# Two-layer short-conv and retention trunk: the engines' order taken from a timeline simulation, and the first head's norm spread eight steps behind its sums

## The chip, the cores and the metric

One core of a Trainium2 chip. The metric is device microseconds (us) of one execution of the whole program. TensorE is called PE here (PEld: its weight loads), VectorE DVE, ScalarE ACT, GpSimd POOL and SyncE SP. The kernel before takes 1546.74 us, the median of 3 runs (1546.3 to 1547.41).

## The reference

x is (1, 512, 1024) in float32; 16 learned rows are put in front of it, which makes T = 528 rows, and taken away at the end. Each of two layers computes:

```python
def layer(h, p):
    u = rmsnorm(h, pre_norm_g) @ w_in + b_in          # 1024 -> 10240 columns
    # a gated short convolution (3 taps) on 4 x 1024 of the columns
    a = (gb * conv(gc * hh) * silu(z)) @ w_conv_out
    # retention: 4 heads, q and k of 256, v and gate of 512 columns each
    out = decayed_scores(rope(q), rope(k)) @ v
    out = group_norm(out) * silu(z_r)                 # per head and row, over 512
    b = out @ w_ret_out
    y = (sigmoid(g_a) * a + sigmoid(g_b) * b) @ w_o
    return h + rmsnorm(y, post_norm_g)
```

The group norm of a head is the step that the change moves: it needs a sum over the head's 512 values for every row, the power -1/2 of it, and that number at every partition before the head's output can be scaled.

## The kernel before, in words

Everything is held transposed: 1024 features lie on partitions as 8 blocks of 128, and the 528 rows are the free dimension, mostly cut in two halves of 264 (HALF). Every product of float32 matrices is made of three matmuls of a high and a low part: a CAST on ACT makes the high part (L140, `whi`, `Xh`, `r`), a subtraction on DVE the low part (L141, `wlo`, `Xl`, `r`), PE multiplies high by high, high by low and low by high. Weights are loaded as `raw` (SP's queue) and split by those same two lines.

Most of w_in's columns go through `Group` (L283 is its matmul): a Strassen-like scheme with 7 products of 12 matmuls, into the PSUM banks `pa`, `pb`, `pc`; DVE adds weight blocks for it (L311, L318, L319), and ACT evicts the banks (L329, L339). The first columns of layer 0 and some of layer 1 go through `Std` (L672): 8 feature blocks times 3 matmuls for each half, 48 matmuls for 128 columns, into a pair of banks that is copied out by L1023 in layer 0. `pp` is a pool of two PSUM pairs that the scores (L425), the transposes of v (L454), the norms (L374, L388) and other products share in turn: a third user waits until the first one's contents have been read.

A head of retention is k and q, rotated by DVE (rope, L407 to L409: two products and an add or a subtraction, `f<-f,f`), split for PE; scores (L425 on PE, times the decay by L436 on DVE, split by L444 and L445); v transposed (L454) and split by L461, L462 and L467; then `attend` (L486), and the norm in three steps: the sums over partitions by matmuls with a column of ones (L374), scaled by DVE (`nv`, L378), raised to -1/2 by POOL (`ny`, L379); the spread over the partitions by a matmul with `ident` (L388), copied out by ACT (L391); and the scaling of the head's output (L520). The first head of each layer starts it with `z_done(...)` at L1071 and L1090, the others inside `Group`'s callbacks.

What sets the order: the program is written as a list of jobs for PE; `later(d, f)` puts a piece of other work d ticks ahead, and every 12 or so matmuls of PE are one tick (`tick()`), at which what is due is issued. For a norm, `d` is the tick of the sums, and the spread was due at `d + 3`, the scaling at `d + 3 + v`. On top of that the framework (`tile.TileContext`, L1298) puts each engine's instructions in its own order when the program is built, by a simulation that starts with the order of the code and lets pieces marked `tc.high_priority()` (evictions mostly) go first. Every engine then runs its list in order, and waits where an input isn't there or a buffer isn't free.

At the layer change, `wo_half` multiplies by w_o (L672, `wos` and `r` as weights), ACT evicts each product as `YB` (L763) and squares it (L663), DVE adds the squares into `ysum` (L665); `norms` takes the sums (L374), spreads them (L388), scales `YB` (L776), adds the residual (L781), squares and sums again into `hsum` (L663, L665), spreads, scales (L785) and splits `YB` into `Xh`, `Xl` or `r`. All that is done for each half of the rows, and `opening` (L672, `pp_10129` and others) begins layer 1 with the result.

Of the kernel before, what the change touches and what calls it, by code (L numbers as in the profile page):

```python
# [56 lines left out]
def trunk(ctx: ExitStack, tc: tile.TileContext, xT, w_in, binT, w_co, w_ro, w_o, gpre, gpost,  # L57
          gpost_row, convw, convb, gng, cosT, sinT, decay, out):
    nc = tc.nc
# [65 lines left out]
    def later(delay, fn):  # L125
        now[1] += 1
        heappush(queue, (now[0] + delay, now[1], fn))
# [690 lines left out]
    jobs, shut = [], [[False], [False]]  # L818
    entry = [[{}, {}], [{}, {}]]
    for l in range(DEPTH):  # L820
# [7 lines left out]
        hd = heads(0)  # L828
# [56 lines left out]
                for j in range(len(JT)):  # L885
                    later(d + 2 * j, lambda j=j: vtrans(vt, hd["v8"], V, (j,)))

        def z_done(ts, hd, h, l, yr, silu=(1,), d=11):
            cs = slice(QCOLS[l].t0, T)
            for n in silu:  # L890
                later(1, lambda n=n: nc.scalar.activation(ts[n][:, cs], ts[n][:, cs], AF.Silu))
            hd["zt"] = hd.get("zt", []) + list(ts)
            if len(hd["zt"]) < 4:
                return

            def start():
                hd["sums"] = fslot()
                hd["n"] = normed(l, hd["zt"], hd["sums"], yr)
            later(0, start)
            for v in range(4):  # L900
                later(1 + 2 * v, lambda v=v: attend(l, h, *hd["S"], hd["V"], v, hd["zt"][v], hd["sums"]))
            later(d, lambda: hd["n"][0]())
            later(d + 3, lambda: hd["n"][1]())
            for v in range(4):
                later(d + 3 + v, lambda v=v: hd["n"][2](v))

        hd["done"] = (k_done, q_done, v_done, z_done)
        yrs = jb["yrs"] = [[] for _ in range(H)]
# [7 lines left out]
        for h in range(1, H):  # L916
            d = {}
# [150 lines left out]
    for b, half, j in ((A11, 0, 0), (A12, 0, 4), (A22, 1, 4)):  # L1068
        for kk in range(0, 4, 2):
            split(Xh[:, b, kk:kk + 2], Xl[:, b, kk:kk + 2], YH[:, j + kk:j + kk + 2, half, :])  # L1070
    later(14, lambda: z_done(zt, jobs[0][0]["hd"], 0, 0, jobs[0]["yrs"][0], (), 16))  # L1071

    for l in range(DEPTH):
        last = l == DEPTH - 1
# [3 lines left out]
        if l:  # L1078
            hd = jb[0]
            k_done(opened[0:2], hd["hd"])  # L1080
            hd["z"][0].run(0, biased_silu)
            block_sums(0)
            hd["z"][0].run(1, biased_silu)
            block_sums(1)
            q_done(opened[6:8], hd["hd"], 0, 1, 12)
            hd["z"][1].run(0, biased_silu)
            v_done(opened[2:6], hd["hd"], 9)
            hd["z"][1].run(1, biased_silu)
            zt = hd["z"][0].ts + hd["z"][1].ts
            later(14, lambda zt=zt: z_done(zt, jobs[1][0]["hd"], 0, 1, jobs[1]["yrs"][0], (), 16))  # L1090
        wo = jb["wo"].wo
        co = 0

# [208 lines left out]
```

## Time and profile before

| | |
|---|---|
| median of 3 runs | 1546.74 us (1546.3 to 1547.41) |
| the profiled execution | 1547.21 us |
| its span, first to last instruction | 1545.1 us |
| mean granted TensorE clock | 0.997 |
| PE busy | 1527.5 us, 99% |
| PEld busy | 1484.1 us, 96% |
| DVE busy | 1164.2 us, 75% |
| ACT busy | 910.5 us, 59% |
| POOL busy | 30.6 us, 2% |

The profile is of one execution. Its own time lies 0.5 us above the median, and its span 2.1 us below its own time. A row of the timeline gives the start, the duration, the engine, the line, the operation, what it writes and reads, how many alike stand in it, and in brackets the idle time before it with what ended that. Instructions of one engine overlap a little, so the step from one row's start to the next is shorter than the duration.

### The profile page before, as it was taken

How to read it: one execution, taken by the hardware profiler on the slowest of the kernel's cores; microseconds unless marked ns; L12 is line 12 of the kernel's file. 1: busy time of each engine (PE TensorE's matmuls, PEld its weight loads, DVE VectorE, ACT ScalarE, POOL GpSimd, SP SyncE). 2: the span in 40 equal slices, each digit the busy share in tenths (PEclk: the TensorE clock that was granted, in tenths of full speed). 3: DMA queues.
4: the chain of work that ended last, by engine and by line, in shares of the span. 5: the costliest groups of instructions: out<-in, count | busy, mean ns of one | idle time of the engine just before them, and what ended most of it. 6: DMA issues, size and time to landing. Idle time of an engine off the chain costs nothing.

```text
span 1545.1 us, 29345 instructions
## 1 busy us (share of the span) xinstructions
PE 1527.5 (99%) x11762; PEld 1484.1 (96%) x11762; DVE 1164.2 (75%) x1702; ACT 910.5 (59%) x1764; POOL 30.6 (2%) x31
## 2 busy tenths in 40 slices
PE   9998999999999999999999999999999999999998
PEld 9998999999999999999999999999999999999986
DVE  6997776886978788856376988769779777997642
ACT  7684666565465466755345766665755655776531
POOL 0001000000000000000000000000000000000000
PEclk9999999999999999999999999999999999999999
DMA  8132223323232334335331233332322223333431
GB/s 273 55 131 89 96 95 105 113 101 103 89 117 89 104 123 137 130 130 181 122 105 55 98 109 110 117 103 96 123 96 100 100 96 123 132 135 138 139 102 55
DMA packets 86041, 174.38 MB, mean 113 GB/s; under 512 B 11281, under 2 KB 15889, under 8 KB 85905
## 3 DMA queue, kind: packets, MB, share of 16 engines
q1 hardware_dynamic: 85760, 172.50, 32.9%
q8 instruction: 92, 1.51, 0.4%
q14 instruction: 45, 0.36, 0.1%
q10 hardware_dynamic: 144, 0.01, 0.0%
HBM read 168.21 MB, written 4.26 MB: 112 GB/s over the span
## 4 chain that ended last, share of the span: by engine, by line
PE 93%; DVE 3%; ACT 1%; DMA 1%; issue 1%; POOL 0%; SPq 0%; DVEq 0%; POOLq 0%; ACTq 0%
PE pb L283 30%; PE pp L248 18%; PE pc L283 15%; PE pp L672 7%; PE pa L283 7%; PE pp L486 4%; PE pb L672 3%; PE pp L425 2%; PE pp L1164 2%; PE pp L454 1%; PE pp L388 1%; DVE wlo L141 1%; DMA raw<-in_w_in 1%; PE pp L374 1%; POOL ny L379 0%
## 5 line engine op out<-in xcount | busy, mean ns | idle before, releaser
L140 ACT CAST whi<-raw 128x1024 fp32r<-128x1024 f32 (+2 forms) x358 | 339.8, 958 | 234.8 <-PE pp L248 62.9
L141 DVE TENSOR_TENSOR wlo<-raw,whi 128x1024 fp32r<-128x1024 f32 (+2 forms) x358 | 393.6, 1107 | 111.8 <-ACT whi L140 110.1
L283 PE MATMUL pb<-Xh,whi 128*128 128x264 f32 (+2 forms) x1008 | 290.7, 288 | 3.1 <-ACT pa L339 1.6
L283 PE MATMUL pb<-Xl,whi 128*128 128x264 f32 (+2 forms) x1008 | 285.7, 283 | 0.0
L283 PE MATMUL pb<-Xh,wlo 128*128 128x264 f32 (+2 forms) x1008 | 285.7, 283 | 0.0
L248 PE MATMUL pp<-r,whi 128*128 128x264 f32 (+1 forms) x1152 | 244.4, 321 | 0.0
L283 PEld LDWEIGHTS pb<-Xh,whi 128*128 128x128 f32 x1008 | 190.4, 189 | 4.8 <-ACT pa L339 2.2
L283 PE MATMUL pc<-Xh,whi 128*128 128x264 f32 (+2 forms) x672 | 192.2, 286 | 0.9 <-ACT f L329 0.9
L248 PEld LDWEIGHTS pp<-r,whi 128*128 128x128 f32 x1152 | 176.8, 188 | 15.4 <-ACT whi L140 0.3
L283 PEld LDWEIGHTS pb<-Xl,whi 128*128 128x128 f32 x1008 | 190.4, 189 | 0.7
L283 PE MATMUL pc<-Xl,whi 128*128 128x264 f32 (+2 forms) x672 | 190.4, 283 | 0.0
L283 PEld LDWEIGHTS pb<-Xh,wlo 128*128 128x128 f32 x1008 | 190.2, 189 | 0.0
L283 PE MATMUL pc<-Xh,wlo 128*128 128x264 f32 (+2 forms) x672 | 190.1, 283 | 0.0
L248 PE MATMUL pp<-r,wlo 128*128 128x264 f32 (+1 forms) x576 | 153.3, 321 | 0.0
L311 DVE TENSOR_TENSOR raw<-raw 128x512 f32<-128x512 f32 x168 | 114.9, 687 | 37.6 <-DMA raw<-in_w_in 35.2
L283 PEld LDWEIGHTS pc<-Xh,whi 128*128 128x128 f32 x672 | 126.5, 188 | 1.5 <-ACT f L329 1.4
L283 PEld LDWEIGHTS pc<-Xl,whi 128*128 128x128 f32 x672 | 126.5, 188 | 0.1
L283 PEld LDWEIGHTS pc<-Xh,wlo 128*128 128x128 f32 x672 | 126.3, 188 | 0.0
L248 PEld LDWEIGHTS pp<-r,wlo 128*128 128x128 f32 x576 | 95.5, 188 | 8.4
L283 PE MATMUL pa<-Xh,whi 128*128 128x264 f32 (+2 forms) x336 | 96.3, 287 | 0.0
L283 PE MATMUL pb<-Xh,whd 128*128 128x264 f32 (+2 forms) x336 | 95.3, 284 | 1.0 <-ACT f L329 1.0
L318 DVE TENSOR_TENSOR raw<-raw,raw 128x512 f32<-128x512 f32 x84 | 57.9, 689 | 50.6 <-DMA raw<-in_w_in 50.2
(257 smaller groups left out, 3335.5 us busy)
## 6 DMA issues: line engine op xcount, KB each, us to landing
raw<-in_w_in SPq DMA_DIRECT2D x426, 256.0 KB, 2.9
raw<-in_w_ro SPq DMA_DIRECT2D x32, 512.0 KB, 3.3
raw<-in_w_in SPq DMA_DIRECT2D x20, 512.0 KB, 5.2
raw<-in_w_co SPq DMA_DIRECT2D x16, 512.0 KB, 3.3
raw<-in_w_o SPq DMA_DIRECT2D x16, 512.0 KB, 4.0
Dsb<-in_decay SPq DMA_DIRECT2D x8, 520.0 KB, 4.6
h1d<-f SPq DMA_DIRECT2D x8, 264.0 KB, 5.6
f<-h1d SPq DMA_DIRECT2D x8, 264.0 KB, 4.3
```

The costliest lines, as they stand in the source:

```text
L140: nc.scalar.copy(dst_hi, src)
L141: nc.vector.tensor_tensor(dst_lo, src, dst_hi.bitcast(F32), op=ALU.subtract)
L248: nc.tensor.matmul(banks[i][:, 0:cols.n], wt(k)[:, msl], xs(k)[:, sl], start=(k == 0 and a == 0), stop=(k == nk - 1 and a == 2),)
L283: nc.tensor.matmul(o[:, 0:n], wt[:, k, :], xs[:, blk, k, HALF - n:], start=(first and k == 0 and a == 0), stop=(k == 3 and a == 2), skip_g ...
L311: nc.vector.tensor_tensor(r[:, 512:], r[:, 512:], r[:, 0:512], op=ALU.add)
L318: nc.vector.tensor_tensor(b[:, 0:512], a[:, 512:], c[:, 0:512], op=ALU.add)
L374: nc.tensor.matmul(pp[0:sc, 0, c:c + 1], sums[:, t0 + c * sc:t0 + (c + 1) * sc], ones_d[:, 0:1], start=True, stop=True)
L388: nc.tensor.matmul(pp[:, c // per, (c % per) * sc:(c % per + 1) * sc], y[:, c:c + 1].to_broadcast([sc, P]), ident[0:sc, 0:sc], start=True, ...
L425: nc.tensor.matmul(pp[0:kn, n + i, 0:cols.n], k[dt][x][:, k0:k0 + kn] if j < 4 else k8[:, dt * 2 + x, :], q[dt][y][:, sl], start=(dt == 0 ...
L486: nc.tensor.matmul(pp[:, b, lo_ - banks[b][0]:hi_ - banks[b][0]], V[j][x][0:kn, v * P:(v + 1) * P], S[0:kn, SOFF[j] + lo_ - q0:SOFF[j] + h ...
L672: nc.tensor.matmul(o, wt(k), xs[:, i0:], start=(k == 0 and a == 0), stop=(k == KD - 1 and a == 2))
L1164: nc.tensor.matmul(o, x[:, xs], wo[k][half][w], start=(k == 0 and a == 0), stop=(k == KD - 1 and a == 2))
```

## The change

`z_done` gets one more argument, `e`, the ticks between a norm's sums and its spread (3 as before if it isn't given). The first heads of both layers are called with sums 13 ticks ahead instead of 16, and the spread 8 ticks behind them instead of 3, so it is due at 21 instead of 19. And `TileContext` is called with `schedule_with_timeline_sim=True`: the framework makes each engine's order by its timeline simulation instead of its default one. This last line moves instructions in the whole program.

```diff
--- before.py
+++ after.py
@@ -885,7 +885,7 @@
                 for j in range(len(JT)):
                     later(d + 2 * j, lambda j=j: vtrans(vt, hd["v8"], V, (j,)))
 
-        def z_done(ts, hd, h, l, yr, silu=(1,), d=11):
+        def z_done(ts, hd, h, l, yr, silu=(1,), d=11, e=3):
             cs = slice(QCOLS[l].t0, T)
             for n in silu:
                 later(1, lambda n=n: nc.scalar.activation(ts[n][:, cs], ts[n][:, cs], AF.Silu))
@@ -900,9 +900,9 @@
             for v in range(4):
                 later(1 + 2 * v, lambda v=v: attend(l, h, *hd["S"], hd["V"], v, hd["zt"][v], hd["sums"]))
             later(d, lambda: hd["n"][0]())
-            later(d + 3, lambda: hd["n"][1]())
+            later(d + e, lambda: hd["n"][1]())
             for v in range(4):
-                later(d + 3 + v, lambda v=v: hd["n"][2](v))
+                later(d + e + v, lambda v=v: hd["n"][2](v))
 
         hd["done"] = (k_done, q_done, v_done, z_done)
         yrs = jb["yrs"] = [[] for _ in range(H)]
@@ -1068,7 +1068,7 @@
     for b, half, j in ((A11, 0, 0), (A12, 0, 4), (A22, 1, 4)):
         for kk in range(0, 4, 2):
             split(Xh[:, b, kk:kk + 2], Xl[:, b, kk:kk + 2], YH[:, j + kk:j + kk + 2, half, :])
-    later(14, lambda: z_done(zt, jobs[0][0]["hd"], 0, 0, jobs[0]["yrs"][0], (), 16))
+    later(14, lambda: z_done(zt, jobs[0][0]["hd"], 0, 0, jobs[0]["yrs"][0], (), 13, 8))
 
     for l in range(DEPTH):
         last = l == DEPTH - 1
@@ -1087,7 +1087,7 @@
             v_done(opened[2:6], hd["hd"], 9)
             hd["z"][1].run(1, biased_silu)
             zt = hd["z"][0].ts + hd["z"][1].ts
-            later(14, lambda zt=zt: z_done(zt, jobs[1][0]["hd"], 0, 1, jobs[1]["yrs"][0], (), 16))
+            later(14, lambda zt=zt: z_done(zt, jobs[1][0]["hd"], 0, 1, jobs[1]["yrs"][0], (), 13, 8))
         wo = jb["wo"].wo
         co = 0
 
@@ -1295,7 +1295,7 @@
     args = [nc.dram_tensor(f"in_{n}", a.shape, mybir.dt.from_np(a.dtype), kind="ExternalInput").ap()
             for n, a in arrays.items()]
     args.append(nc.dram_tensor("out_y", (SEQ, D), F32, kind="ExternalOutput").ap())
-    with tile.TileContext(nc) as tc:
+    with tile.TileContext(nc, schedule_with_timeline_sim=True) as tc:
         trunk(tc, *args)
     r = run_bass_kernel_spmd(nc, [{f"in_{n}": a for n, a in arrays.items()}], core_ids=[0])
     return r.results[0]["out_y"].reshape(1, SEQ, D)
```

**The first head's norm, on PE.** `ones_d` against `f` are the sums, `ny` is the spread, the L283 rows are products of `Group`. Before:

```order
L374 MATMUL pp_1936<-ones_d,f_1525 88x1 x6
L283 MATMUL pb_1885<-Xh,whi_1787 128x264
...
L283 MATMUL pa_104<-Xh,whi_1787 128x264
...
L283 MATMUL pc_1886<-Xh,whi_1839 128x264
...
L283 MATMUL pc_1886<-Xh,wlo_1840 128x264
L388 MATMUL pp_2009<-ident,ny_1944 128x88 x6
L283 MATMUL pb_1885<-Xh,whi_1839 128x264
```

and now:

```order
L374 MATMUL pp_1875<-ones_d,f_1525 88x1 x6
L283 MATMUL pb_1896<-Xh,whi_1721 128x264
...
L283 MATMUL pc_1897<-Xh,whi_1721 128x264
...
L283 MATMUL pb_1729<-Xh,whd_1661 128x264
...
L283 MATMUL pb_1729<-Xh,wld_1662 128x264
L388 MATMUL pp_2046<-ident,ny_1883 128x88
L283 MATMUL pb_1896<-Xh,whi_1787 128x264
...
L283 MATMUL pb_2031<-Xh,wlo_1889 128x264
L388 MATMUL pp_2046<-ident,ny_1883 128x88 x5
L283 MATMUL pc_2032<-Xh,whi_1888 128x264
```

Before and now, 36 matmuls of L283 stand between the sums and the first matmul of the spread; now the other five of the spread stand 60 matmuls further down. (A line of "..." leaves out rows of the same product.)

**The first head's rope, on ACT and DVE.** `f_778` and `f_795` are the two rotated halves of k, `pp_765` the PSUM pair with the second half of the columns of q. ACT before:

```order
L1027 ACTIVATE f_408<-f_408,bin_92 128x528
L1027 ACTIVATE f_411<-f_411,bin_92 128x528
L140 CAST whi_928<-raw_513 128x1024
L140 CAST r_812<-f_778 128x528
L140 CAST r_828<-f_795 128x528
L1023 COPY f_843<-pp_765 128x264 x2
L1027 ACTIVATE f_414<-f_414,bin_92 128x528
L1027 ACTIVATE f_518<-f_518,bin_92 128x528
```

ACT now:

```order
L140 CAST Xh<-f_690 128x528
L140 CAST whi_995<-raw_516 128x1024
L1027 ACTIVATE f_758<-f_758,bin_92 128x528
L140 CAST r_812<-f_778 128x528
L140 CAST r_828<-f_795 128x528
L140 CAST whd_1286<-t_1214 128x512
L1023 COPY f_843<-pp_765 128x264 x2
L396 CAST r_869<-r_812 128x128
```

DVE before, up to the second rotated half:

```order
L407 TENSOR_TENSOR f_795<-f_408,sin_sb 128x528
L409 TENSOR_TENSOR f_778<-f_778,f_779 128x528
L408 TENSOR_TENSOR f_796<-f_411,cos_sb 128x528
L141 TENSOR_TENSOR wlo_833<-raw_449,whi_832 128x512
L409 TENSOR_TENSOR f_795<-f_795,f_796 128x528
L141 TENSOR_TENSOR r_813<-f_778,r_812 128x528
L1026 TENSOR_TENSOR f_414<-f_414,f_457 128x528
```

DVE now:

```order
L408 TENSOR_TENSOR f_796<-f_411,cos_sb 128x528
L318 TENSOR_TENSOR raw_838<-raw_677,raw_840 128x512
L141 TENSOR_TENSOR Xl<-f_688,Xh 128x528
L1026 TENSOR_TENSOR f_758<-f_758,f_457 128x528
L311 TENSOR_TENSOR raw_840<-raw_840 128x512
L141 TENSOR_TENSOR Xl<-f_689,Xh 128x528
L141 TENSOR_TENSOR Xl<-f_690,Xh 128x528
L409 TENSOR_TENSOR f_778<-f_778,f_779 128x528
L311 TENSOR_TENSOR raw_999<-raw_999 128x512
L409 TENSOR_TENSOR f_795<-f_795,f_796 128x528
L319 TENSOR_TENSOR t_1214<-raw_838 128x512
L141 TENSOR_TENSOR wlo_996<-raw_516,whi_995 128x1024
```

The casts of both rotated halves still stand ahead of the copy that empties `pp_765`, and one more cast (`whd_1286`) with them. On DVE, work that stood behind the second rotated half (weight sums of later groups, the product of `f_758` with the norm) now stands ahead of it: 14 instructions more in all, of which five are of L1026, two of L318, four of L311, one of L319 and two of L141.

**The layer change, on ACT and DVE.** `pb_9595`, `pb_9596` and `pp_9653` are the last three products of w_o's second half; `f_9646` and `f_9650` are squares of the first two, `f_9711` and `f_9715` of the third; L378 belongs to the sums of `hsum`, which PE takes behind `pp_9653`. ACT before:

```order
L663 ACTIVATE f_9592<-pp_9495 128x264
L663 ACTIVATE f_9646<-pb_9595 128x264
L663 ACTIVATE f_9650<-pb_9596 128x264
L140 CAST Xh<-raw_9212 128x512
L140 CAST Xh<-raw_9214 128x512
L763 ACTIVATE YB<-pp_9653,gpost_sb 128x264
L663 ACTIVATE f_9711<-pp_9653 128x264
L763 ACTIVATE YB<-pp_9653,gpost_sb 128x264
L663 ACTIVATE f_9715<-pp_9653 128x264
```

ACT now:

```order
L663 ACTIVATE f_9592<-pp_9495 128x264
L763 ACTIVATE YB<-pp_9653,gpost_sb 128x264
L663 ACTIVATE f_9646<-pb_9595 128x264
L663 ACTIVATE f_9650<-pb_9596 128x264
L663 ACTIVATE f_9711<-pp_9653 128x264
L763 ACTIVATE YB<-pp_9653,gpost_sb 128x264
L663 ACTIVATE f_9715<-pp_9653 128x264
```

DVE before:

```order
L665 TENSOR_TENSOR ysum<-ysum,f_9646 128x264
L665 TENSOR_TENSOR hsum<-hsum,f_9582 128x264
L665 TENSOR_TENSOR ysum<-ysum,f_9650 128x264
L665 TENSOR_TENSOR hsum<-hsum,f_9586 128x264
L141 TENSOR_TENSOR Xl<-raw_9212,Xh 128x512
L141 TENSOR_TENSOR Xl<-raw_9214,Xh 128x512
L378 TENSOR_SCALAR nv_9706<-pp_9702 88x3
L665 TENSOR_TENSOR ysum<-ysum,f_9711 128x264
L665 TENSOR_TENSOR ysum<-ysum,f_9715 128x264
```

DVE now:

```order
L665 TENSOR_TENSOR ysum<-ysum,f_9646 128x264
L665 TENSOR_TENSOR hsum<-hsum,f_9574 128x264
L665 TENSOR_TENSOR ysum<-ysum,f_9650 128x264
L665 TENSOR_TENSOR hsum<-hsum,f_9578 128x264
L665 TENSOR_TENSOR ysum<-ysum,f_9711 128x264
L665 TENSOR_TENSOR hsum<-hsum,f_9582 128x264
L665 TENSOR_TENSOR ysum<-ysum,f_9715 128x264
L665 TENSOR_TENSOR hsum<-hsum,f_9586 128x264
L378 TENSOR_SCALAR nv_9706<-pp_9702 88x3
```

The two squares of `pb` stand behind the eviction of `pp_9653` now, and the four additions to `ysum` stand between those to `hsum`, ahead of the norm's sums.

Two more moves there and one in the heads, in words. DVE now issues all eight L785 and three splits of `raw` before the first split of the new `YB` (before: four L785, then four splits of `YB`). On PE, 10 matmuls stand between the second half's sums (`pp_10036`) and its spread (`pp_10068`) and none between the spread and the products that need it (before: 24 and 24). And in the later heads, PE's order around the scores was 12 of L425, 12 of L283, 4 of L454, 12 of L283, 12 of L425; now the L425, L454 and L425 follow each other with 0 to 3 matmuls of L283 between them, in six of the eight heads.

## Rows read from the trace of the kernel before

**Rows 1.** The page, part 1: busy us, share of the span, instructions.

```profile
PE 1527.5 (99%) x11762; PEld 1484.1 (96%) x11762; DVE 1164.2 (75%) x1702; ACT 910.5 (59%) x1764; POOL 30.6 (2%) x31
```

**Rows 2.** PE's waits in the whole span: us in total, times, longest.

```profile
PE pp L388 <- POOL ny L379: 4.8, 1, 4.8
PE pb L283 <- ACT f L1023: 1.4, 1, 1.4
```

**Rows 3.** Timeline of PE around the first head's norm.

```profile
142.83 1.03 PE L374 MATMUL pp<-ones_d,f 128*88 128x1 f32 x12
...
153.11 2.86 PE L388 MATMUL pp<-ident,ny 88*128 88x88 f32 x12 [4.77 <-POOL ny L379]
...
156.06 0.42 PE L283 MATMUL pb<-Xl,whi 128*128 128x264 f32 x1
...
158.04 0.42 PE L283 MATMUL pb<-Xl,whi 128*128 128x264 f32 x1
```

**Rows 4.** Windows: us, busy of PE, PEld, DVE, ACT, POOL, then PEclk, DMA share, GB/s.

```profile
60.00:80.00 20.00, 20.00 (x166) 20.00 (x165) 20.00 (x31) 15.10 (x29) 0.00 (x0) 1.00 0.23 79
84.00:88.00 4.00, 3.57 (x26) 3.34 (x26) 3.87 (x7) 4.00 (x10) 0.00 (x0) 1.00 0.00 0
154.00:158.00 4.00, 4.00 (x20) 4.00 (x20) 1.35 (x3) 1.59 (x3) 0.00 (x0) 0.50 0.02 7
```

**Rows 5.** Timeline of POOL: the powers of the first two heads.

```profile
147.22 5.84 POOL L379 TENSOR_TENSOR ny<-nv,mhalf 88x6 f32<-88x6 f32 x1 [17.30 <-DVE nv L378]
...
272.17 2.20 POOL L379 TENSOR_TENSOR ny<-nv,mhalf 88x6 f32<-88x6 f32 x1 [7.05 <-DVE nv L378]
```

**Rows 6.** Timeline of DVE around the first head's norm.

```profile
144.56 0.69 DVE L318 TENSOR_TENSOR raw<-raw,raw 128x512 f32<-128x512 f32 x1 [1.82 <-DMA raw<-in_w_in]
...
146.92 0.15 DVE L378 TENSOR_SCALAR nv<-pp 88x6 f32<-88x6 f32 x1
```

**Rows 7.** Timeline of DVE around the first head's rope.

```profile
64.71 0.70 DVE L1026 TENSOR_TENSOR f<-f,f 128x528 f32<-128x528 f32 x1
65.33 1.22 DVE L141 TENSOR_TENSOR wlo<-raw,whi 128x1024 fp32r<-128x1024 f32 x1
```

**Rows 8.** Timeline of ACT there.

```profile
63.50 0.65 ACT L1023 COPY f<-pp 128x264 f32<-128x264 f32 x2
```

**Rows 9.** Timeline of PE there: two blocks of 48 begin.

```profile
66.96 0.29 PE L672 MATMUL pp<-Xh,whi 128*128 128x264 f32 x1
...
72.81 0.29 PE L672 MATMUL pb<-Xh,whi 128*128 128x264 f32 x1
```

**Rows 10.** Timeline of PE at the layer change.

```profile
782.68 0.56 PE L374 MATMUL pp<-ones_d,hsum 128*88 128x1 f32 x6
...
786.58 0.80 PE L388 MATMUL pp<-ident,ny 88*128 88x88 f32 x6
...
790.17 0.28 PE L672 MATMUL pb<-Xh,whi 128*128 128x264 f32 x1
```

**Rows 11.** Timeline of ACT at the layer change.

```profile
782.88 0.48 ACT L763 ACTIVATE YB<-pp,gpost_sb 128x264 f32<-128x264 f32 x1 [2.51 <-PE pp L672]
783.26 0.38 ACT L663 ACTIVATE f<-pp 128x264 f32<-128x264 f32 x1
```

**Rows 12.** Timeline of DVE at the layer change.

```profile
784.33 0.43 DVE L665 TENSOR_TENSOR ysum<-ysum,f 128x264 f32<-128x264 f32 x1 [0.22 <-ACT f L663]
787.83 1.71 DVE L785 SCALAR_TENSOR_TENSOR YB<-f,gpre_sb,f 128x264 f32<-128x264 f32 x4 [3.06 <-ACT f L391]
789.45 1.46 DVE L141 TENSOR_TENSOR Xl<-YB,Xh 128x264 fp32r<-128x264 f32 x4
```

**Rows 13.** Timeline of DVE in a later head.

```profile
223.15 1.22 DVE L141 TENSOR_TENSOR wlo<-raw,whi 128x1024 fp32r<-128x1024 f32 x1 [0.19 <-ACT whi L140]
224.29 1.01 DVE L436 TENSOR_TENSOR f<-pp,Dsb 128x448 f32<-128x448 f32 x2
```

**Rows 14.** Timeline of ACT in that head.

```profile
222.08 1.04 ACT L140 CAST whi<-raw 128x1024 fp32r<-128x1024 f32 x1
```

## The prediction

> **What bounds the kernel now.** I read the page first, to see which engine has no room: PE is busy for 99% of the span, DVE for 75% and ACT for 59% [rows 1]. So an order can gain only what PE waits now, and can lose whatever it makes PE wait anew. PE's waits come next: the largest is one of 4.8 us for the power of the first head's norm, and the next one that matters is 1.4 us for an eviction by L1023 [rows 2]. The timeline of PE shows what the large one costs besides itself: it begins at 153.11 - 4.77 = 148.34, the spread then takes until about 155.7, and from 156.06 to 158.04 nine matmuls step by 0.22 us each [rows 3], where the usual step is (72.81 - 66.96) / 48 = 0.122 [rows 9]. The windows name the reason: the granted clock is 0.50 there, the 1.2 GHz level, while it stayed at 1.00, 2.4 GHz, behind the wait of 1.4 us at 83.6 [rows 4]. The twelve spread matmuls last 2.6 us in place of the 1.2 that two spreads of six would take at 0.58 each, and the eleven or so slow ones of L283 lose 0.1 each: 2.6 us on top of the wait. The last reading is the order that each engine has now: where a release of PE moved behind other work, I priced that work by rows.
>
> **First head's norm: -5.5 us.** The change asks for eight ticks between sums and spread, but in the new order only five of the six spread matmuls stand further down; the first stands 36 matmuls behind the sums, as before. That is 36 x 0.122 = 4.4 us of cover. What is needed is the scaling on DVE, 0.3 us until POOL starts, and the power. Before, the scaling ran at 146.92 [rows 6], some 3 us behind the sums, because a weight sum that waited 1.82 us for its load, and two more instructions, stood ahead of it; then POOL needed 5.84 us, against 2.20 for the same shape in the next head [rows 5]. In the new order the scaling stands ahead of that weight sum (`raw_1794`), so I let it run at once: 0.3 + 5.84 - 4.4 leaves a wait of 1.8 us. The clock should hold, as it did behind 1.4 us [rows 4]. So 4.8 + 2.6 us become about 1.9: -5.5. Bounds: with a power of 2.20 us there is no wait (-7.4); with the scaling as late as before nothing is gained (0). I stay with 5.84, since DVE has two-input work ready behind the scaling in both orders.
>
> In the Trainium skill, "SBUF — State Buffer", section "SBUF: two separate sides", a DVE instruction with two SBUF inputs and a GpSimd instruction that reads SBUF exclude each other for a whole instruction. The 5.84 us fit that in direction, and by the rule with an idle DVE this term would be -7.4. No row here shows the same power with DVE idle in that place.
>
> **First head's rope: +6.4 us.** The block of 48 that PE begins at 66.96 takes over the PSUM pair of `pp_765`, which ACT has to copy out first. That copy stood at 63.50 [rows 8], just behind the casts of the rotated k, and 3.5 us ahead of the block [rows 9]. Now 14 more DVE instructions precede the last rope addition: twelve of about 0.61 us (the step from 64.71 to 65.33, which is 0.08 less than the duration), one of 1.14 (1.22 less 0.08) and one of 0.6 [rows 7], 9.0 us in all; DVE is busy for 20.00 of 20 us there [rows 4], with no gap that could absorb them. ACT gains one cast of 0.5. The copy ends at 63.50 + 0.65 + 9.0 + 0.5 = 73.7, PE arrives at 66.96 plus twelve matmuls of another product that stand ahead of the block now, 1.5 us, so at 68.4: a wait of 5.3 us. That is as long as the 4.8 us that halved the clock, so 2.6 more; and the present wait of 1.4 us [rows 2] comes too late to remain: -1.5. Bounds: 0, if the work ahead of this stretch ends earlier by as much; 10, if the next copies, which stand behind it, are late again.
>
> **Entry, first 30 us: +3 us.** ACT casts two feature blocks in a row, so the third weight part of one comes behind two scalings and two casts of the next. PE would wait some 1 us in three places. Bounds 0 and 4, because the loads set part of the pace there.
>
> **Layer change: +10.4 us.** Three places.
> - Sums of `hsum`. PE reaches them at 782.68 [rows 10]. Now eight DVE additions stand behind the square of `pb_9595`, and that square behind the eviction of `pp_9653`, which ran at 782.88 [rows 11]. The square is there at 783.26 + 0.38; eight additions of 0.35 (0.43 less the 0.08 of overlap) [rows 12] end at 786.4: PE waits 3.7 us, where it had nothing to wait for at the sums.
> - First split of the new `YB`. Four L785 of 1.62 / 4 = 0.405 and three splits of 0.6 now stand ahead, 3.4 us. Before, that split ended near 789.9 [rows 12], 0.3 ahead of its use at 790.17 [rows 10]; with a few matmuls that PE can still do, 2.9 us.
> - Second half. The 24 matmuls behind the spread are gone. From spread to first L785 it takes 787.83 - 786.58 = 1.25 us [rows 10, 12], then eight L785 (3.2) and one split (0.4); the spread itself and four matmuls cover 1.1: 3.8 us. Before, three L785 stood ahead, and 24 x 0.122 = 2.9 us of cover hid them.
> Bounds: 3 (only the first holds, and the rest is hidden by loads and banks) and 13 (each with a little clock loss).
>
> **Later heads: +12 us.** Where L425, L454 and L425 follow each other, the second L425 block needs the pair of the first, which DVE empties by L436: 1.01 us for the two, perhaps behind a weight split of 1.22 [rows 13], against some 0.5 us of transposes: 0.5 to 1.7 us, say 1.1, in six heads: 6.6. Evictions of `Group` by L329 now stand behind a cast of 1.04 [rows 14] once in five of the heads, 1 us each: 5. Bounds 0 (the cover is elsewhere) and 16.
>
> **Sum.** -5.5 + 3 + 6.4 + 10.4 + 12 = +26.3. Nothing else is charged: PE's matmuls and the loads stay the same, and SP's list hardly moves, so the transfers start as now wherever their buffers come free as now. The profiled execution of 1547.2 becomes 1573.5; it stands 0.5 above the median, so 1573 us.
>
> **The rivals.**
> - *Hidden after all (faster).* DVE and ACT are free for 25% and 41% of the time [rows 1]; if DVE drains its inserted work before the rope inputs arrive, so that each release still comes before PE asks, only the first head's gain stays: 1546.7 - 5.5 = 1541. It decides whether the copy of `pp_765` ends before 68.4. Against it: the rope chain and the norm chains are in-order lists whose stretches I priced as full. 6%.
> - *No effect.* The timeline simulation gives back elsewhere what it takes here, within 3 us, which is the 0.2% that a measurement of this kernel can tell: 1544 to 1550. For it there is only the unchanged amount of work. 4%.
> - *Only the single places.* The heads hide their part by waiting where they already had a spare bank: 1573 - 12 = 1561. 20%.
> - *The clock falls at each new wait.* The waits of 5.3, 3.7, 2.9 and 3.8 us are all longer than the 1.4 that left the clock at 1.00 [rows 4]; I charged only the first. If the other three and the first head's cost 2.6 each as well: 1573 + 10.4 = 1583. 15%.
>
> The Trainium skill, "TensorE: Matmul & The Clock Gate", section "HAM oscillation — how this bites in real kernels", says that a wait between groups of matmuls is paid again as slow matmuls after each of them. The 154:158 window agrees, the 84:88 window does not show it; it is the last rival, with 1583 by the rule.
>
> **How the numbers follow.** The sum is likeliest, with 55%. The range reaches down to the single places, 1560, and up past the clock rival, 1588, since the heads' bound of 16 and the layer change's 13 can meet it; it leaves out the 10% of the two cases at or below the present time and the far ends. Faster by more than 0.2%: 0.06, within: 0.04, slower: 0.90.
>
> **What would show it.** In the changed profile, PE's wait for the power should be under 2 us, a wait of some 5 us for L1023 should stand near 70 to 80 us, with a lower granted clock behind it, PE should wait 3 to 4 us at the `hsum` sums, at the first L672 of the opening and behind the second spread, and L425 should wait for L436 in most heads. PE's idle total should be near 45 us where it was 17.6. The prediction is wrong if that total stays under 25 us, or if PE's busy time itself changes by more than the clock loss.

## The result, and the profile after

The changed kernel takes 1583.69 us, the median of 4 runs (1582.09 to 1584.42), where the kernel before takes 1547.05 (4 runs): 36.6 us slower, ratio 1.0236, 95% interval 1.0218 to 1.0254. The forecast was 1573, with a range of 1560 to 1588.

The page of the changed kernel, its span, part 1 and the clock's row of part 2 (mean share in 40 slices of the span); [rows 1] stand against the second line:

```profile
span 1582.3 us, 29393 instructions
PE 1542.2 (97%) x11762; PEld 1496.0 (95%) x11762; DVE 1164.1 (74%) x1702; ACT 908.8 (57%) x1764; POOL 25.6 (2%) x31
PEclk9999999999999999999989999999999999999999
```

The span grew by 37.2 us. PE's idle time grew from 1545.1 - 1527.5 = 17.6 us to 1582.3 - 1542.2 = 40.1, by 22.5; the other 14.7 us are PE's own busy time, with the same 11762 matmuls. DVE, ACT and POOL did no more work than before.

PE's nine largest waits in the whole span (us in total, times, longest), against [rows 2]:

```profile
PE pp L425 <- DVE f L436: 5.0, 4, 1.9
PE pp L672 <- ACT f L1023: 4.9, 2, 3.8
PE pp L374 <- DVE hsum L665: 3.8, 1, 3.8
PE pc L283 <- ACT f L329: 3.1, 3, 1.7
PE pb L283 <- ACT f L329: 2.9, 4, 0.8
PE pb L672 <- DVE Xl L141: 2.6, 1, 2.6
PE pp L672 <- ACT whi L140: 2.4, 4, 1.0
PE pp L672 <- ACT f L1015: 1.6, 1, 1.6
PE pp L672 <- ACT f L814: 1.6, 1, 1.6
```

The wait for the power, 4.8 us in [rows 2], is gone. In its place stand waits for copies, splits, sums and evictions, from every part of the program. (L329, L814 and L1015 are evictions on ACT like L1023, of other products.)

PE issues the same matmuls in both kernels, so the lag can be read off at equal work: the time at which PE has issued the same number of columns, after less before. Between two marks the lag's growth is what that stage cost.

| stage, by the time before | lag at its end, us | its cost | forecast |
|---|---|---|---|
| entry, to 34 us | 4.2 | +4.2 | +3 |
| rope, to 98 us | 11.9 | +7.8 | +6.4 |
| first head's norm, to 166 us | 4.6 | -7.3 | -5.5 |
| rest of layer 0, to 748 us | 7.1 | +2.5 | with the heads |
| layer change, to 839 us | 22.5 | +15.4 | +10.4 |
| heads of layer 1, to 1316 us | 34.9 | +12.4 | +12 |
| the rest, to 1536 us | 37.3 | +2.3 | with the heads |

So the places were the forecast ones. Windows of the changed kernel (us, busy of PE, PEld, DVE, ACT, POOL, then PEclk, which is the granted clock as a share of 2.4 GHz, DMA share, GB/s) at the rope, the first head's norm, and the sums of `hsum`:

```profile
66.00:86.00 20.00, 14.69 (x84) 14.26 (x85) 20.00 (x31) 8.76 (x19) 0.00 (x0) 0.75 0.19 66
66.00:72.00 6.00, 4.44 (x24) 4.23 (x25) 6.00 (x10) 3.18 (x7) 0.00 (x0) 0.76 0.46 162
80.00:86.00 6.00, 5.33 (x24) 5.33 (x25) 6.00 (x10) 2.10 (x8) 0.00 (x0) 0.50 0.12 44
140.00:160.00 20.00, 20.00 (x170) 20.00 (x170) 16.34 (x24) 11.84 (x21) 2.34 (x2) 1.00 0.35 119
793.00:800.00 7.00, 6.23 (x32) 6.26 (x33) 0.78 (x3) 0.00 (x0) 0.85 (x1) 0.53 0.00 0
800.00:841.00 41.00, 35.34 (x265) 34.47 (x264) 24.37 (x58) 15.68 (x43) 1.84 (x3) 0.92 0.28 99
```

PEclk is what the forecast undercounted: 0.75 in the rope's 20 us, 0.53 behind the sums, 0.92 over the rest of the layer change. In the heads it is 0.57 from 236 to 240 us, behind a wait of 1.25 us, and 0.52 from 1127 to 1134, behind one of 1.92. At the first head's norm it is 1.00 now, where the kernel before had 0.50 behind its wait [rows 4]. Timeline of PE at the rope and at the layer change, with the idle time and its end in brackets:

```profile
66.46 0.39 PE L283 MATMUL pc<-Xh,whi 128*128 128x264 f32 x1 [1.02 <-ACT whi L140]
...
68.07 0.39 PE L672 MATMUL pp<-Xh,whi 128*128 128x264 f32 x1 [1.10 <-ACT f L1023]
...
80.67 0.59 PE L672 MATMUL pp<-Xh,whi 128*128 128x264 f32 x1 [3.75 <-ACT f L1023]
```

```profile
793.77 1.01 PE L374 MATMUL pp<-ones_d,hsum 128*88 128x1 f32 x6 [3.82 <-DVE hsum L665]
...
799.87 0.80 PE L388 MATMUL pp<-ident,ny 88*128 88x88 f32 x6
...
806.65 0.59 PE L672 MATMUL pb<-Xl,whi 128*128 128x264 f32 x1 [2.65 <-DVE Xl L141]
```

```profile
832.99 0.90 PE L388 MATMUL pp<-ident,ny 88*128 88x88 f32 x6
...
835.33 0.39 PE L672 MATMUL pp<-r,whi 128*128 128x264 f32 x1 [1.44 <-ACT r L140]
...
837.29 0.59 PE L672 MATMUL pp<-r,whi 128*128 128x264 f32 x1 [1.58 <-ACT f L814]
```

The waits at the layer change, 3.82, 2.65 and 1.44 + 1.58, stand against 3.7, 2.9 and 3.8 worked out beforehand; that at the rope is 3.75 at the copy of `pp_765` and 1.10 at the one before it, against 5.3 for the copy of `pp_765` alone.

How the wait at the sums comes about is seen in ACT (first) and DVE (second) there, against [rows 11, 12]:

```profile
781.60 2.17 ACT L140 CAST Xh<-raw 128x512 fp32r<-128x512 f32 x4
...
788.83 0.39 ACT L663 ACTIVATE f<-pp 128x264 f32<-128x264 f32 x1 [0.52 <-DVE hsum L665]
789.99 0.48 ACT L763 ACTIVATE YB<-pp,gpost_sb 128x264 f32<-128x264 f32 x1 [0.76 <-PE pp L672]
790.37 0.66 ACT L663 ACTIVATE f<-pb 128x264 f32<-128x264 f32 x2
```

```profile
790.78 0.43 DVE L665 TENSOR_TENSOR ysum<-ysum,f 128x264 f32<-128x264 f32 x1 [0.75 <-ACT f L663]
...
793.19 0.43 DVE L665 TENSOR_TENSOR hsum<-hsum,f 128x264 f32<-128x264 f32 x1
```

Four casts of the opening's weights run in one go at 781.60, ahead of the squares; those of the two `pb` come at 790.37, behind the eviction of the last product; DVE stands idle for 0.75 us until the first is there, and the last addition ends at 793.62, which releases PE at 793.77. That the casts are what pushes the squares back is tried in e5.

### The profile page after: what moved, and what is told of

It is laid out like the page before. It is cut to its first block, busy times and chain, and to the rows that moved or that the text cites. A ratio compares the mean times of both kernels' runs of the same rounds, so it can differ in the third digit from the quotient of the medians.

```text
span 1582.3 us, 29393 instructions
## 1 busy us (share of the span) xinstructions
PE 1542.2 (97%) x11762; PEld 1496.0 (95%) x11762; DVE 1164.1 (74%) x1702; ACT 908.8 (57%) x1764; POOL 25.6 (2%) x31
## 4 chain that ended last, share of the span: by engine, by line
PE 89%; DVE 4%; ACT 3%; DMA 2%; issue 1%; SPq 0%; DVEq 0%; POOLq 0%; ACTq 0%
PE pb L283 29%; PE pp L248 16%; PE pc L283 14%; PE pa L283 7%; PE pp L672 7%; PE pp L486 5%; PE pb L672 3%; PE pp L1164 2%; PE pp L425 2%; DMA raw<-in_w_in 2%; DVE wlo L141 1%; ACT whi L140 1%; PE pp L388 1%; PE pp L454 1%; PE pp L374 1%
## 5 line engine op out<-in xcount | busy, mean ns | idle before, releaser
L140 ACT CAST whi<-raw 128x1024 fp32r<-128x1024 f32 (+2 forms) x358 | 339.6, 959 | 283.8 <-PE pp L248 63.8
L141 DVE TENSOR_TENSOR wlo<-raw,whi 128x1024 fp32r<-128x1024 f32 (+2 forms) x358 | 393.0, 1108 | 134.7 <-ACT whi L140 131.5
L283 PE MATMUL pb<-Xh,whi 128*128 128x264 f32 (+2 forms) x1008 | 289.3, 288 | 2.9 <-ACT f L329 2.9
L283 PE MATMUL pb<-Xl,whi 128*128 128x264 f32 (+2 forms) x1008 | 286.3, 284 | 0.0
L283 PE MATMUL pb<-Xh,wlo 128*128 128x264 f32 (+2 forms) x1008 | 285.9, 284 | 0.0
L248 PE MATMUL pp<-r,whi 128*128 128x264 f32 (+1 forms) x1152 | 246.9, 321 | 0.3 <-ACT whi L140 0.3
L283 PE MATMUL pc<-Xh,whi 128*128 128x264 f32 (+2 forms) x672 | 191.9, 286 | 4.1 <-ACT f L329 3.1
L283 PEld LDWEIGHTS pb<-Xh,whi 128*128 128x128 f32 x1008 | 190.4, 189 | 5.1 <-ACT f L329 3.9
L283 PEld LDWEIGHTS pb<-Xl,whi 128*128 128x128 f32 x1008 | 190.7, 189 | 1.0
L248 PEld LDWEIGHTS pp<-r,whi 128*128 128x128 f32 x1152 | 177.3, 188 | 14.5 <-ACT whi L140 0.5
L283 PE MATMUL pc<-Xl,whi 128*128 128x264 f32 (+2 forms) x672 | 191.0, 284 | 0.0
L283 PEld LDWEIGHTS pb<-Xh,wlo 128*128 128x128 f32 x1008 | 190.4, 189 | 0.4
L283 PE MATMUL pc<-Xh,wlo 128*128 128x264 f32 (+2 forms) x672 | 190.4, 283 | 0.0
L248 PE MATMUL pp<-r,wlo 128*128 128x264 f32 (+1 forms) x576 | 152.4, 321 | 0.0
L311 DVE TENSOR_TENSOR raw<-raw 128x512 f32<-128x512 f32 x168 | 115.5, 687 | 49.6 <-DMA raw<-in_w_in 47.6
L283 PEld LDWEIGHTS pc<-Xh,whi 128*128 128x128 f32 x672 | 126.5, 188 | 5.8 <-ACT f L329 3.7
L283 PEld LDWEIGHTS pc<-Xl,whi 128*128 128x128 f32 x672 | 126.5, 188 | 0.5
L283 PEld LDWEIGHTS pc<-Xh,wlo 128*128 128x128 f32 x672 | 126.4, 188 | 0.2
L248 PEld LDWEIGHTS pp<-r,wlo 128*128 128x128 f32 x576 | 95.3, 188 | 7.8
L329 ACT ACTIVATE f<-pb,bin 128x264 f32<-128x264 f32 (+2 forms) x186 | 82.6, 454 | 29.3 <-PE pb L283 29.3
L318 DVE TENSOR_TENSOR raw<-raw,raw 128x512 f32<-128x512 f32 x84 | 57.9, 689 | 53.2 <-DMA raw<-in_w_in 53.0
L283 PE MATMUL pa<-Xh,whi 128*128 128x264 f32 (+2 forms) x336 | 96.4, 287 | 0.0
```

The source lines that it names most:

```text
L140: nc.scalar.copy(dst_hi, src)
L141: nc.vector.tensor_tensor(dst_lo, src, dst_hi.bitcast(F32), op=ALU.subtract)
L248: nc.tensor.matmul(banks[i][:, 0:cols.n], wt(k)[:, msl], xs(k)[:, sl], start=(k == 0 and a == 0), stop=(k == nk - 1 and a == 2),)
L283: nc.tensor.matmul(o[:, 0:n], wt[:, k, :], xs[:, blk, k, HALF - n:], start=(first and k == 0 and a == 0), stop=(k == 3 and a == 2), skip_g ...
L311: nc.vector.tensor_tensor(r[:, 512:], r[:, 512:], r[:, 0:512], op=ALU.add)
L318: nc.vector.tensor_tensor(b[:, 0:512], a[:, 512:], c[:, 0:512], op=ALU.add)
```

## The experiments

Eleven kernels in three groups; each group shares its runs of the kernel before. "Held in order" means `tc.keep_in_program_order(...)` around an instruction: the framework may not let it pass anything on its engine that is written ahead of it. It adds no work.

**The two halves of the change, each alone.**

```diff
 # e1: the kernel before with
-    with tile.TileContext(nc) as tc:
+    with tile.TileContext(nc, schedule_with_timeline_sim=True) as tc:
 # e2: the changed kernel with that line as before (sums at 13, spread 8 behind)
```

> The kernel before with the timeline-simulated order alone; the norm's sums and spread stay at 16 and 19 ticks. Theory A, the new order costs at the entry, the rope, the layer change and the later heads, and the first head's wait goes away wherever some 40 matmuls stand between sums and spread: in this order 40 stand there (4.9 us), so a power of 2.2 us leaves no wait and one of 5.84 us leaves 1.2 us: 1583 to 1586 us, PE waits for the power 0 to 1.2 us. Theory B, the spacing is what removed the first head's wait: that wait of 4.8 us and the 2.6 us of slow clock come back on top of the changed kernel: 1591 us.

> The kernel before with the first heads' sums at 13 and spread 8 ticks behind them, in the default order. There 96 matmuls (11.7 us) stand between sums and spread. Theory A, the wait of 4.8 us and the 2.6 us of slow clock behind it are all that the norm cost: 1547.0 - 7.4 = 1539.6 us, no wait for the power. Theory C, the later spread delays the scaling of the head and what needs it, so that another wait takes its place: 1545 to 1550 us.

e1: 1585.63 us (ratio 1.0252, 1.0230 to 1.0274). PE has no wait for the power, which takes 2.87 us:

```profile
156.13 2.87 POOL L379 TENSOR_TENSOR ny<-nv,mhalf 88x6 f32<-88x6 f32 x1 [14.71 <-DVE nv L378]
```

The lag against the changed kernel stays within 0.6 us but for one stretch of layer 1, where it is 3 us and comes back. Theory A: the whole loss is the order's, and the first head's wait goes away by the order too. The two intervals overlap, so in the new order the moved norm is worth nothing that can be told.

e2: 1539.43 us (0.9949, 0.9933 to 0.9966): -7.4 would have been 1539.6. Timeline of PE (the spread) and POOL there:

```profile
151.61 1.47 PE L388 MATMUL pp<-ident,ny 88*128 88x88 f32 x12
```

```profile
141.54 2.80 POOL L379 TENSOR_TENSOR ny<-nv,mhalf 88x6 f32<-88x6 f32 x1 [11.11 <-DVE nv L378]
```

The spread lasts 1.47 us in place of 2.86 [rows 3] and waits for nothing. Theory A again; no other wait took its place. In the default order the norm's move alone is a gain.

**Work that runs too early on DVE.**

```diff
 # e3: the changed kernel, in Group.halves, Group.sums and with_r
-                nc.vector.tensor_tensor(r[:, 512:], r[:, 512:], r[:, 0:512], op=ALU.add)
+                tc.keep_in_program_order(nc.vector.tensor_tensor(r[:, 512:], r[:, 512:], r[:, 0:512], op=ALU.add))
...
-        nc.vector.tensor_tensor(t, t, R, op=ALU.mult)
+        tc.keep_in_program_order(nc.vector.tensor_tensor(t, t, R, op=ALU.mult))
```

> The changed kernel, with the weight sums on DVE (L311, L318, L319) and the products with the norm of layer 0 (L1026) held behind everything that is written ahead of them in the code. Theory A, what makes PE wait at the rope and in the later heads is DVE work on later weights that runs too early: the rope's 7.8 us and some 8 to 10 us of the heads go: 1564 to 1568 us, while the layer change keeps its three waits of 3.8, 2.6 and 3.0 us. Theory D, PE's own order (L425 next to L454 and L425) makes the heads wait, and DVE's does not matter there: 1574 to 1577 us; if neither matters 1584 us.

1562.32 us (1.0095, 1.0078 to 1.0112): 21.4 us of the 36.6 come back with nothing done but holding four kinds of DVE instruction; theory A's range, 1564 to 1568, is passed by 1.7 us. Against the changed kernel, the lag falls by 6.0 us up to 141 us (by 10 up to 98, of which 4 are lost again behind a wait of 2.46 us for an eviction by L339 at 102.11), by 4.1 in the second head of layer 0, and by 8 in the heads of layer 1; at the layer change it does not move (-0.2). The waits for L436 are gone from PE's list, and the layer change's stand as they were (behind the second spread another of 1.4 us goes with the last row):

```profile
PE pp L374 <- DVE hsum L665: 3.8, 1, 3.8
PE pb L672 <- DVE Xl L141: 2.7, 1, 2.7
PE pp L672 <- ACT f L814: 1.6, 1, 1.6
```

What the early weight sums do in a head is seen in DVE of the changed kernel, in its second head, and in PE beside it:

```profile
231.71 0.69 DVE L311 TENSOR_TENSOR raw<-raw 128x512 f32<-128x512 f32 x1
232.32 1.22 DVE L141 TENSOR_TENSOR wlo<-raw,whi 128x1024 fp32r<-128x1024 f32 x1
233.45 1.02 DVE L436 TENSOR_TENSOR f<-pp,Dsb 128x448 f32<-128x448 f32 x2
```

```profile
230.68 2.25 PE L425 MATMUL pp<-r,r 128*128 128x448 f32 x12
232.76 0.60 PE L454 MATMUL pp<-ident,f 128*128 128x128 f32 x4
234.62 1.50 PE L425 MATMUL pp<-r,r 128*128 128x192 f32 x12 [1.25 <-DVE f L436]
```

A weight sum and a weight split stand ahead of the pair of L436, which could have begun at 232.9, where L425's block ends; it begins at 233.45 and ends at 234.47, and the next L425, which takes over the same PSUM pair, waits 1.25 us. Some 0.5 of it are due to the sum and the split; the rest comes from PE being there so soon. In e3 the pair follows PE at once, and the simulation, which orders all engines anew, has also put some 20 matmuls of L283 between L425 and L454: so e3 tells what held sums are worth in the whole, not DVE from PE in the heads.

**PE's own order.**

```diff
 # e4: the changed kernel, at all eleven places where PE is called
-                nc.tensor.matmul(o, wt(k), xs[:, i0:], ...)
+                tc.keep_in_program_order(nc.tensor.matmul(o, wt(k), xs[:, i0:], ...))
```

> The changed kernel with all matmuls and transposes of PE held in the order of the code; DVE and ACT are still ordered by the timeline simulation. Theory D, PE's own order makes the later heads wait (13 us) and takes the cover from the layer change's second half (3 us): 1568 to 1574 us. Theory A, the late releases on DVE and ACT decide, and PE only arrives at them: 1584 us or more, up to 1593, with PE's waits on DVE and ACT as large as in the changed kernel.

1591.99 us (1.0283, 1.0263 to 1.0303), 8.3 us slower than the changed kernel, at the far end of what theory A allowed. It is not all of one sign: 4.1 us are won in the second head of layer 0, and some 12 in the heads of layer 1, which is what theory D expected for the heads. But 7 us are lost up to 511 us and 8.2 near 1300, where PE waits at L248 for splits by DVE and ACT (the longest 2.55 us), and 6.8 up to 766, half of it a wait of 3.55 us for an eviction by L329. In the second head of layer 0 a weight split still stands ahead of the pair of L436 in e4 (it begins at 227.69, the pair at 228.83), and PE does not wait: 24 matmuls of L283 and the transposes stand between the two blocks of L425 again, as before the change. So there the lost cover on PE is needed for the wait; as e4 too has all engines ordered anew, what DVE's lateness adds in the heads was not separated from it.

**The layer change.**

```diff
 # e5: the changed kernel, in Std.halves, for the weights of the opening
-                split(hi, lo, self.raw[j]["raw"][:, a:a + 512])
+                part = self.raw[j]["raw"][:, a:a + 512]
+                if ring:
+                    split(hi, lo, part)
+                    continue
+                tc.keep_in_program_order(nc.scalar.copy(hi, part))
+                tc.keep_in_program_order(nc.vector.tensor_tensor(lo, part, hi.bitcast(F32), op=ALU.subtract))
```

> The changed kernel, with the splits of the weights that the opening of layer 1 uses (casts on ACT, subtractions on DVE) held behind everything that is written ahead of them. Theory A, these casts run too early on ACT, push the squares behind the eviction of w_o's last product, and so make PE wait 3.8 us at the sums of hsum: that wait falls under 1 us, and with the slow matmuls behind it 4 to 6 us go: 1577.5 to 1580 us; the waits for the new YB (2.6) and behind the second spread (3.0) stay. Theory E, only DVE's own order of additions makes it, or PE merely waits at the next place instead: 1582 to 1585 us.

1577.95 us (1.0207, 1.0191 to 1.0222), 5.7 us below the changed kernel, with three runs at 1577.1 to 1578.4 and one at 1582.34. PE at the sums, at the block behind them, and at the first new `YB`:

```profile
790.75 0.60 PE L374 MATMUL pp<-ones_d,hsum 128*88 128x1 f32 x6 [0.19 <-DVE hsum L665]
792.06 0.51 PE L672 MATMUL pp<-r,Xh 128*128 128x264 f32 x2 [0.71 <-ACT f L663]
...
800.42 0.39 PE L672 MATMUL pb<-Xl,whi 128*128 128x264 f32 x1 [1.22 <-DVE Xl L141]
```

3.82 us have become 0.19 + 0.71, as theory A had it. It had 2.65 stay, but that became 1.22, since three of the held splits stood ahead of that one too. The lag falls by 8.3 us in this stretch: 2.9 and 1.4 are the two waits, and the other 4 are mostly matmuls that are not slow any more.

```diff
 # e6: e3 and e5 together, and the matmuls of ktiles, rstd_token and spread held in order
-                nc.tensor.matmul(o, wt(k), xs[:, i0:], start=(k == 0 and a == 0), stop=(k == KD - 1 and a == 2))
+                tc.keep_in_program_order(nc.tensor.matmul(o, wt(k), xs[:, i0:], start=(k == 0 and a == 0), stop=(k == KD - 1 and a == 2)))
```

> The changed kernel with three things held in the order of the code: the weight sums on DVE as in the third run, the opening's splits as in the fifth, and PE's matmuls of Std, w_o, the opening and the norms; the rest of all engines is ordered by the timeline simulation. Theory A, the loss is made of a few groups of instructions that run too early, and these three hold most of it: from 1562.3 us down by the layer change's 15 us to 1545 to 1551 us. Theory F, as with all of PE held in order, other waits take their place: 1556 us or more.

1553.69 us (1.0043, 1.0026 to 1.0060), between the two theories: 30.0 of the 36.6 us are back, and the rest has moved rather than stayed: a new wait of 2.2 us for a power stands at the layer change, at 794.10. Against e2, which has the same norm in the default order, 14 us remain: 3 at the entry, 8 at the layer change and 5 in the heads of layer 1, less 2 that are won at the rope. What holds these was not tried.

**What made the first head wait.**

```diff
 # e7: e2 with the spread 3 ticks behind the sums        # e9: e2 with the sums at 16
-... jobs[0]["yrs"][0], (), 13, 8))                      -... (), 13, 8))
+... jobs[0]["yrs"][0], (), 13))                         +... (), 16, 8))
```

> The kernel before, in the default order, with the first heads' sums at 13 ticks in place of 16 and the spread still 3 ticks behind them: 36 matmuls (4.4 us) between them, as before. Theory G, the power was long (5.84 us) because of the place in DVE's work in which it ran, and at 13 ticks it lasts 2.8 us as in the second run: no wait, 1539 to 1541 us, so the eight ticks are not needed. Theory A, the spacing is what covers it: the power is long again or the scaling late, PE waits 1.5 to 4.8 us: 1541.5 to 1547 us.

> The kernel before, in the default order, with the first heads' sums left at 16 ticks and the spread 8 ticks behind them: 96 matmuls (11.7 us) between them, and behind the scaling on DVE the same seven instructions without a pause as before. Theory L, the power's last 1.2 us begin only where DVE pauses: it lasts 5.8 us or more again, but the 96 matmuls cover it: no wait of PE, 1539 to 1541 us. Theory M, the 5.84 us were an accident of one execution: the power lasts 2.2 to 2.9 us here, with the same total. If spacing does not cover it, PE waits at the spread and the time is 1543 us or more.

e7: 1541.20 us (0.9964, 0.9951 to 0.9977); e9: 1540.11 (0.9955, 0.9943 to 0.9968). Timelines of POOL and of PE at the spread, e7 first:

```profile
140.60 2.80 POOL L379 TENSOR_TENSOR ny<-nv,mhalf 88x6 f32<-88x6 f32 x1 [10.85 <-DVE nv L378]
```

```profile
143.63 1.47 PE L388 MATMUL pp<-ident,ny 88*128 88x88 f32 x12
```

```profile
148.01 5.84 POOL L379 TENSOR_TENSOR ny<-nv,mhalf 88x6 f32<-88x6 f32 x1 [17.84 <-DVE nv L378]
```

```profile
156.45 1.47 PE L388 MATMUL pp<-ident,ny 88*128 88x88 f32 x12
```

Either half of the norm's move is enough, in two ways. With the sums earlier the power is short, and 36 matmuls cover it (theory G, though 0.2 us above its range; a wait of 1.46 us for an eviction by L339 is new behind the spread); with the spread later the power is as long as before, 5.84 us to the hundredth, and 96 matmuls cover it (theory L).

```diff
 # e8: e2, and behind the sigmoids of both gates (in the kernel by way of a helper, L373)
+                for c in range(2):
+                    nc.gpsimd.tensor_tensor(junk[0:88, :], ts[1][0:88, cs.start + 6 * c:cs.start + 6 * c + 6], mhalf[0:88, :], op=ALU.pow)
```

> The second run's kernel with 32 more powers of 88x6 on POOL, two behind every sigmoid of the gates, whose results nothing reads; it measures how long such a power lasts beside DVE. Theory L, a DVE instruction with two SBUF inputs and the power exclude each other: powers that meet unbroken DVE work for over 2.2 us last 4 us or more, those beside an idle DVE 2.2 or less. Theory M, the power lasts 2.2 to 2.9 us whatever DVE does, as in the changed kernel's first head, and the 5.84 us are an exception: all 32 between 1.7 and 3 us. The time stays at 1538 to 1541 us in both.

1540.54 us in one run. The view of the line that issues the 32 powers (ns: shortest, median, longest):

```profile
L373 POOL TENSOR_TENSOR junk<-f,mhalf x32: 1316/1573/2291, 617.5 to 1467.5; 88x6 f32<-88x6 f32 x32
```

None is long. The longest, 2.29 at 627.99, began beside work of DVE that went on without a pause for 2.9 us behind its start, where theory L has 4 us or more: L fails here. Theory M's range, 1.7 to 3 us, is not met either: the median is 1.57. The shortest, 1.32 us, stand beside an idle DVE, but the two from 713.50 on took 1.33 and 1.32 as well, with DVE at its splits nearly all the time. In e9 the power was as long as L has it. So neither theory holds for both runs.

**A version beside the best one.** e10 is e2 once more, beside e9; e11 gives the L1023 copies high priority:

```diff
     def raw_out(d, o, m):
-        nc.scalar.copy(d, o)
+        with tc.high_priority():
+            nc.scalar.copy(d, o)
```

> The second run's kernel once more, beside the ninth and eleventh, to compare three neighbours by one and the same set of runs: 1539 to 1540 us, power 2.8 us, no wait for it.

> The second run's kernel with the copies of layer 0's first products (L1023) given high priority: the one PE wait of 1.4 us for such a copy at 83.6 us should go. If nothing takes its place 1538 us; if the casts that now stand behind the copies come late instead, 1539.4 us or more.

e10: 1539.02 us (0.9949, 0.9936 to 0.9961). e11: 1539.60 (0.9952, 0.9939 to 0.9966): the wait of 1.4 us is halved to 0.7, but 1.4 us for casts (`pp L672 <- ACT whi L140`) take its place. Nothing is gained. The best version seen is the norm's move in the default order, 0.5% faster than the kernel before; e7, e9 and e11 cannot be told from it.

## Why the prediction was right, and where its terms were off

The sign, the places and the mechanism held; the sum, +26.3, was 10.3 us short of the 36.6. The waits that it added up came out smaller by 4 us (idle time +22.5, where its terms make +26); the clock, which it put at nothing on balance, cost 14.7.

- **What bounds.** PE had no room, and the waits came through in the time: PE's idle time is 40.1 us, where 45 were forecast. The rival that DVE and ACT would hide it, by their 25% and 41% of free time, fell: DVE, idle for 26% of the time, makes PE wait by the order of its instructions with no more work than before, as the changed kernel against e3 shows. The rival in which the heads hide their part fell with the 12.4 us of layer 1.
- **First head's norm, -5.5; measured -7.3.** The mis-sized term is the power: "I stay with 5.84". It took 2.20 us, so no wait was left, which was the lower bound of that term. The step that failed is the reason given for 5.84, DVE's work behind the scaling; in the changed kernel DVE was busy with such work throughout (rows in the last section), and the power was short. That the first spread matmul stands no further behind the sums than before was right, and e1 shows that the new order takes the wait away without the eight ticks.
- **Rope, +6.4; measured +7.8.** The copy of `pp_765` was late through the casts and the L409 ahead of it, as worked out. The wait was 3.75 in place of 5.3, but both of its ends lay far from the forecast: the copy ended at 80.61, where 73.7 was worked out, and PE was there at 80.67 - 3.75 = 76.92, where 68.4 was. PE came with the lag of the entry, 4.2 us, and had waited 1.0 and 1.1 us more at 66.46 and 68.07, with a lower clock behind; none of that was in the term. That the two shifts nearly cancel is luck. e3 shows the cause for most of this stage's loss.
- **Entry, +3; measured +4.2.** Waits of 0.95, 0.45, 0.78 and 1.60 us for casts and a copy of L1015; three of about 1 us were forecast. No run tried its cause; e6 keeps 3 us of it.
- **Layer change, +10.4; measured +15.4.** The waits were 3.82, 2.65 and 3.02 for 3.7, 2.9 and 3.8 forecast: 9.5 for 10.4. The rest, some 6 us, is mostly the clock, which this term did not charge. e5 shows the chain from the early casts over the squares to the sums.
- **Heads, +12; measured 17.2 with the end of the program.** Both mechanisms are in PE's list: L425 for L436, 5.0 us in 4 waits, in four of the eight heads where six were priced at 6.6, and evictions by L329, 6.0 us in 7, where the kernel before had 1.9. With 2.4 us for L467, which wasn't priced, the new waits are some 11.5 us, about the +12; most of the rest is the clock from 236 and from 1127 us on, which this term did not charge either. Layer 1 took nearly all; in layer 0 only the second head lost much (4.1), and the others were as before or better.
- **The clock.** "I charged only the first" is the step that was wrong by most. PE's busy time rose by 14.7 us with the same matmuls, although the 2.6 us of slow matmuls at the first head were gone. The granted clock was 0.53 behind the wait of 3.82, and 0.75 in the rope's window, where two waits of 1.0 and 1.1 us came before the long one. The rival with the clock at each new wait gave 1583 us, which is the measured time; it was one of four with 15%. That it met the time so closely is luck in part: it had 10.4 us of clock where 14.7 came, and the same waits, too long by 4 us. Nor did its condition, a wait longer than 1.4 us, set the places apart: the clock was lower behind 1.25 us at 234.62, and stayed at 1.00 behind 1.60 at 27.77 and 1.40 at 1233.91.

By the Trainium skill, "TensorE: Matmul & The Clock Gate", section "HAM oscillation — how this bites in real kernels", the waits between groups of matmuls are paid a second time in each group behind. The windows above agree at 793 and at 66 to 86 us, and the mean clock fell from 0.997 to 0.989; from 27 to 36 and from 1233 to 1242 us, behind the waits of 1.60 and 1.40, it is 1.00 and does not show it.

## What to carry to other kernels

An engine that is idle a quarter of the time still sets the pace if work that nobody needs yet stands ahead of what releases the bound engine; an automatic order has to be read for that, at each place where a PSUM buffer is handed on. A change of several parts is worth trying part by part: here the order lost 2.5% by itself, and the norm's move gained 0.5%. Where the bound engine waits, look at its clock behind each wait and add what it loses there: here 14.7 us of slow matmuls came with 22.5 us of waits, though not behind every one.

## What the runs showed of the hardware

The power of 88x6 on POOL lasted between 1.32 and 5.84 us in these runs. Where DVE's work beside it was the same, in the kernel before and in e9, it took 5.84 us both times. DVE beside the long one in e9, the last row of an unbroken series and the one behind its pause:

```profile
151.97 0.70 DVE L141 TENSOR_TENSOR r<-f,r 128x528 fp32r<-128x528 f32 x1
152.87 1.23 DVE L141 TENSOR_TENSOR wlo<-raw,whi 128x1024 fp32r<-128x1024 f32 x1 [0.20 <-ACT whi L140]
```

The power ends at 148.01 + 5.84 = 153.85, 1.18 us behind the end of that series at 152.67. In the kernel before it ended at 153.06, and a series of the same seven instructions at 151.87; in e2 and e7, 1.2 us behind a pause of DVE as well. 1.2 us is nearly what a power takes beside an idle DVE. So it looks as if the power got its turn where DVE stopped. That is argued and not shown: in the changed kernel's first head it ended after 2.20 us with DVE never pausing, 1.19 us behind the end of one long split:

```profile
151.66 1.23 DVE L141 TENSOR_TENSOR wlo<-raw,whi 128x1024 fp32r<-128x1024 f32 x1
152.80 0.70 DVE L360 TENSOR_TENSOR f<-f,f 128x528 f32<-128x528 f32 x1
```

```profile
151.88 2.20 POOL L379 TENSOR_TENSOR ny<-nv,mhalf 88x6 f32<-88x6 f32 x1 [9.90 <-DVE nv L378]
```

By the Trainium skill, "SBUF — State Buffer", section "SBUF: two separate sides", a DVE instruction with two SBUF inputs and a GpSimd one that reads SBUF exclude each other. The long power agrees; that of 2.20 us beside DVE's unbroken two-input work, and the two of e8 from 713.50 on, do not show it. What made the power long stays open.
